# One ring of split weights for three stages, at the left end of the memory

## The chip, the cores and the metric

The kernel runs on one core of one Trainium2 chip. The metric is device time in microseconds (us) of one execution, as the median of several runs. Engines: PE (matmul), DVE (vector), ACT (scalar), POOL (GpSimd) and SP, which here only issues transfers. Each engine takes its instructions strictly in the order in which the program holds them.

## The reference, cut to what matters

One decoder layer over x of 1024 tokens by 1024 channels, all in float32:

```python
x = layer_norm(ALPHA * x + 0.5 * swiglu(x, ffn1_w_gate, ffn1_w_up, ffn1_w_down), ...)
mix = token_mixer(x, w_in, ...)          # mLSTM branch and RWKV-7 branch, merged by gates
#   inside: merged = sigmoid(gate_a) * y_a + sigmoid(gate_b) * y_b;  return merged @ w_out
x = layer_norm(ALPHA * x + mix, ln2_g, ln2_b)
x = layer_norm(ALPHA * x + 0.5 * swiglu(x, ffn2_w_gate, ffn2_w_up, ffn2_w_down), ...)
# swiglu(x, g, u, d) = (silu(x @ g) * (x @ u)) @ d, inner width 2816
```

## The kernel before

Every float32 product is made of three matmuls on numbers split into a high and a low part: a helper casts a loaded tile to its high part on ACT (L131) and subtracts that from the tile to get the low part on DVE or POOL (L135). The results go into tiles named wr. The change concerns the last three of the program's stages and the ends between them:

- D, the end of the token mixer (`mix`): each product reads split weights w or wf and is evicted by DVE (L1108, L1123), from tiles v, to DRAM (mgD).
- O, the out projection (`down_all` with w_out): three rounds over token groups (0 to 2, 3 to 5, 6 and 7), each with 8 steps. A step loads a slice of the input (hr) and two weight tiles (rw), splits them into six wr tiles, ACT for the high and DVE for the low parts, and runs 6 matmuls for each token tile in it: 18 in a step of three token tiles, 12 in the last round. At its end come the layer norms, on tiles u, and `put_sums`: PE transposes seven combinations of each finished pair of token tiles (L213), ACT and DVE split them (L216, L217) into the parts of x, the tiles xT and xq.
- the second gate stage (`gate_rest`): 22 steps f over the inner width. A step forms combinations of four weight tiles on DVE (L256, tiles tw), splits seven of them into 14 wr tiles (ACT high, POOL low), and runs seven products of 12 matmuls. The step f = 0 takes its tokens in two halves: 14 products of 12 matmuls on 256 columns. Evictions go through tiles e (DVE L277, L300, L304; ACT L288, L292, L299) to DRAM (h2, L285).
- F, the second down stage (`down_all` again): three rounds of 22 steps like those of O, then the last layer norms.

Tiles come from pools, and a pool's memory is given anew when it is closed. Left pools grow upward from low addresses, right pools downward from high ones. A tile whose memory overlaps that of older tiles waits for the last use of each of these. Which pool holds the wr ring (14 buffers of 2 KB per partition) is set by `net.wp`. Before the change there were three rings on the right: one inside O's pool, from 133.4 to 161.4 KB; one in the pool W2 of the gate stage, from 133.9 to 161.9 KB, below the e ring at 161.9 to 189.9 KB; one inside F's pool, from 137.4 to 165.4 KB. So the first ring lay partly over D's tiles v (127.9 to 139.9 KB), the second over the first and half a kilobyte of O's tile lng, the third over the second and two tiles e. In O and F `down_all` first draws one wr tile that nothing uses (`if self.wp is self.sp`).

The order of instructions on each engine, SP's transfers included, is made at build time by a scheduler that estimates when each instruction could start; so a wait for memory that the scheduler foresees also moves instructions. That the three cuts of the weights w, wf lie at 83.8 to 119.8 KB matters for the change.

Of the kernel before, what the change touches and what calls it, by code (L numbers as in the profile page):

```python
# [1134 lines left out]
def build(tc, ins, out):  # L1135
    with ExitStack() as ctx:
        net = Net(ctx, tc, ins, out)
        nc = tc.nc
        net.consts()
        x1D, x2D = (net.dp.tile([T, D], F32, tag=n, name=n) for n in ("x1D", "x2D"))  # L1140
        net.yrD, net.mbD, net.mgD = net.dram("yrD", 1024), net.dram("mbD", 1024), net.dram("mgD", 1024)
        row = lambda tt: slice(tt * P, (tt + 1) * P)

        x1T, gbb = [], []

        def hook1():
            gbb.extend((net.bcast_row(ins["ln1_g"], "lng"), net.bcast_row(ins["ln1_b"], "lnb")))
            net.consts2()

        def fin1(tt, y):  # L1150
            if tt % 4 == 0:
                x1T.append(net.new_xT())
            net.layer_norm(tt, y, *gbb, lambda t: done1(t, y))

        def done1(tt, y):
            nc.sync.dma_start(x1D[row(tt), :], y[tt])
            net.to_T(y[tt], tt, x1T)


        ctx.enter_context(net.pool("pad", "right")).tile([P, 8], F32, tag="pad", bufs=1, name="pad")  # L1160
        x, h1, h2 = ins["x"][0], net.dram("h1", DFF), net.dram("h2", DFF)
        gx, gw, xs = ExitStack(), ExitStack(), ExitStack()
        with net.rings("R1"):
            with net.pool("W1") as net.wp, net.pool("X1") as xp, net.pool("E1", "right") as net.ep:
                d = net.big(xp)
                s4 = d[:, 0:4], d[:, 4:8]
                (a22, s1), (s3, a12), (s2, a11) = (net.halves([net.big(xp) for _ in range(2)]) for _ in range(3))
                ahead = net.gate_first("ffn1", x, [a11, a12, s2, s3, s1, a22, s4], h1)
            gx.enter_context(net.shared("gx", ("xT",)))
            gw.enter_context(net.shared("gw", [t for t in net.GLOBAL if t != "xT"]))  # L1170
            with net.phase("A", UB=6, side="right"):
                net.wp = net.sp
                net.down_all(ins["ffn1_w_down"][0], NF, x, h1, fin1, hook1, ahead)

        middle(net, ins, x1T, x1D)
        gw.close()

        gb2, gb3 = [], []
        c2 = slice(0, 512), slice(512, 1024)

        def rows(v):
            return net.bcast_row(ins[v + "_g"], "lng"), net.bcast_row(ins[v + "_b"], "lnb")

        def fin2(tt, y):
            net.layer_norm(tt, y, *gb2, lambda t: done2(t, y))

        def done2(tt, y):
            nc.sync.dma_start(x2D[row(tt), :], y[tt])
            if tt % 2:
                net.put_sums(cmb, tt // 2, *([t[:, c] for c in c2] for t in y[tt - 1:tt + 1]), net.ring("tw"), "ad")  # L1190

        with net.rings("R2"):
            xp = xs.enter_context(net.pool("X2"))
            (a11, a12), (s2, s3) = (net.halves(net.new_xT()) for _ in range(2))
            s1, a22 = net.halves([net.big(xp) for _ in range(2)])
            d = net.big(xp)
            cmb = [a11, a12, s2, s3, s1, a22, (d[:, 0:4], d[:, 4:8])]
            with net.phase("O", UB=5, side="right"):
                net.wp = net.sp
                net.down_all(ins["w_out"][0], NK, x1D, net.mgD, fin2, lambda: gb2.extend(rows("ln2")))  # L1200
            with net.pool("E2", "right") as net.ep, net.pool("W2", "right") as net.wp:
                ahead = net.gate_rest("ffn2", cmb, h2, 0)
            xs.close()
            with net.phase("F", UB=6, side="right"):
                gb3.extend(rows("ln3"))
                net.wp = net.sp
                net.down_all(ins["ffn2_w_down"][0], NF, x2D, h2,
                             lambda tt, y: net.layer_norm(tt, y, *gb3, lambda t: nc.sync.dma_start(out[0, row(t), :], y[t])),
                             None, ahead)
        gx.close()  # L1210
# [93 lines left out]
```

## Time and profile before

| what | us |
|---|---|
| median of 3 runs | 3240.15 |
| lowest and highest run | 3233.46, 3247.55 |
| the profiled execution, its time | 3242.34 |
| its span, first to last instruction | 3240.3 |
| end of D to the second step of O | 2396.3 to 2405.0 |
| end of O to the second step of the gate stage | 2501.1 to 2561.7 |
| end of the gate stage to the second step of F | 2971.6 to 2987.1 |

Times of rows are us from the start of the span. A row of the timeline gives start, length, engine, line, operation, tiles written and read, and a count; in brackets the idle time before it and who ended it. Rows of matmuls overlap a little, so the pace is read from start to start. PEclk in a row of a stretch is the granted clock of PE as a share of full speed.

### The profile page before, as it was taken

What the parts mean: (1) busy time and instruction counts of PE and PEld (TensorE: products, weight loads), DVE (VectorE), ACT (ScalarE), POOL (GpSimd) and SP (SyncE); (2) the same over time, 40 slices, a digit from 0 to 9 for tenths busy, and PEclk for the clock granted to TensorE, in tenths of its full rate; (3) what the DMA queues carried; (4) which work ended last, traced back from release to release, by engine and by line L of the source; (5) the groups of instructions that cost most, each with busy time, mean ns of one, the idle gap of its engine ahead of it and who ended that gap; (6) DMA issues with size and microseconds to landing.
All of it is one profiled execution on the core that took longest, in us unless ns stands there. A gap on an engine that the chain in (4) does not pass through costs nothing. (4 is left out here: it accounts for less than half of the span.)

```text
span 3240.3 us, 45588 instructions
## 1 busy us (share of the span) xinstructions
PE 3077.5 (95%) x15888; PEld 2496.7 (77%) x15888; DVE 1908.0 (59%) x4812; ACT 1097.3 (34%) x1836; POOL 757.8 (23%) x819
## 2 busy tenths in 40 slices
PE   7999999999999999999999999999998799999997
PEld 6888878877777777787877777777776688887886
DVE  7444435583557676757667766476549544443557
ACT  4333324453213131313222222376334333332444
POOL 4444420022222222222222122200000444442000
PEclk9999999999989999999999999999999899999999
DMA  4332336662222222222232333474675232223665
GB/s 132 93 85 78 86 115 217 190 209 72 64 56 67 74 78 67 76 66 68 60 75 70 75 87 82 144 230 152 191 264 183 80 86 78 78 82 110 203 205 184
DMA packets 497389, 373.81 MB, mean 115 GB/s; under 512 B 110941, under 2 KB 415751, under 8 KB 497159
## 3 DMA queue, kind: packets, MB, share of 16 engines
q1 hardware_dynamic: 488135, 357.26, 37.2%
q0 software_dynamic: 4608, 8.39, 1.0%
q10 hardware_dynamic: 4416, 5.24, 0.5%
q8 instruction: 125, 2.05, 0.3%
q14 instruction: 105, 0.86, 0.1%
HBM read 287.43 MB, written 83.36 MB: 114 GB/s over the span
## 5 line engine op out<-in xcount | busy, mean ns | idle before, releaser
L151 PE MATMUL psg<-xT,wf 128*128 128x512 f32 x2352 | 640.6, 409 | 1.6 <-DVE h L1108 0.9
L151 PEld LDWEIGHTS psg<-xT,wf 128*128 128x128 f32 x2352 | 429.0, 191 | 78.2 <-ACT wf L131 1.3
L131 ACT CAST wr<-rw 128x512 fp32r<-128x512 f32 x444 | 273.2, 621 | 490.5 <-PE psc L151 276.7
L135 DVE TENSOR_TENSOR wr<-rw,wr 128x512 fp32r<-128x512 f32 x312 | 215.5, 697 | 197.2 <-ACT wr L131 186.5
L151 PE MATMUL psa<-xT,w 128*128 128x512 f32 x1200 | 318.5, 408 | 7.5 <-DVE pj L480 4.6
L135 POOL TENSOR_TENSOR wr<-tw,wr 128x512 fp32r<-128x512 f32 x176 | 229.9, 1308 | 248.9 <-ACT wr L131 234.9
L135 POOL TENSOR_TENSOR wr<-rw,wr 128x512 fp32r<-128x512 f32 x132 | 173.4, 1314 | 481.9 <-ACT wr L131 481.7
L151 PE MATMUL psg<-wr,wr 128*128 128x512 f32 x936 | 253.4, 398 | 23.5 <-DVE wr L135 13.3
L151 PEld LDWEIGHTS psa<-xT,w 128*128 128x128 f32 x1200 | 223.7, 193 | 59.5 <-DVE pj L480 9.3
L277 DVE TENSOR_TENSOR e<-psb,e 128x512 f32<-128x512 f32 (+1 forms) x138 | 92.1, 667 | 288.2 <-PE psb L151 288.2
L151 PE MATMUL psb<-xq,wr 128*128 128x512 f32 (+1 forms) x1104 | 257.7, 382 | 4.1 <-DVE e L277 1.7
L151 PE MATMUL psc<-xq,wr 128*128 128x512 f32 (+1 forms) x1104 | 258.7, 383 | 1.6 <-DVE e L277 1.5
L151 PE MATMUL psb<-wr,wr 128*128 128x512 f32 x936 | 250.5, 395 | 0.0
L151 PEld LDWEIGHTS psb<-xq,wr 128*128 128x128 f32 x1104 | 202.1, 189 | 45.3 <-issue 2.1
L151 PEld LDWEIGHTS psc<-xq,wr 128*128 128x128 f32 x1104 | 201.8, 188 | 44.1 <-DVE e L277 1.7
L151 PEld LDWEIGHTS psg<-wr,wr 128*128 128x128 f32 x936 | 175.8, 190 | 69.0 <-DVE wr L135 20.7
L131 ACT CAST wr<-tw 128x512 fp32r<-128x512 f32 x176 | 109.0, 621 | 307.0 <-PE psb L151 219.6
L151 PEld LDWEIGHTS psb<-wr,wr 128*128 128x128 f32 x936 | 178.1, 191 | 37.3
L135 POOL TENSOR_TENSOR w<-raw,w 128x512 fp32r<-128x512 f32 (+1 forms) x51 | 65.5, 1297 | 491.5 <-ACT w L131 429.9
L135 POOL TENSOR_TENSOR wf<-rawf,wf 128x512 fp32r<-128x512 f32 x98 | 130.0, 1342 | 169.6 <-ACT wf L131 154.0
L151 PE MATMUL psc<-wr,wr 128*128 128x512 f32 x624 | 160.1, 391 | 0.0
L758 POOL TENSOR_SCALAR S<-S,PC 128x128 f32<-128x128 f32 x120 | 80.2, 668 | 294.4 <-DVE S L760 180.5
(345 smaller groups left out, 5109.8 us busy)
## 6 DMA issues: line engine op xcount, KB each, us to landing
rw<-in_ffn_w_down_dram SPq DMA_DIRECT2D x264, 256.0 KB
rawf<-in_w_in_dram SPq DMA_DIRECT2D x98, 256.0 KB
rw<-in_ffn_w_gate_dram SPq DMA_DIRECT2D x88, 256.0 KB
rw<-in_ffn_w_up_dram SPq DMA_DIRECT2D x88, 256.0 KB
h<-e SPq DMA_DIRECT2D x80, 256.0 KB
hr<-h SPq DMA_DIRECT2D x88, 192.0 KB
raw<-in_w_in_dram SPq DMA_DIRECT2D x50, 256.0 KB
rw<-in_w_out_dram SPq DMA_DIRECT2D x48, 256.0 KB
```

The lines of the kernel that those rows point to most:

```text
L131: nc.scalar.copy(hi, src)
L135: eng.tensor_tensor(lo, src, hi.bitcast(F32), op=ALU.subtract)
L151: self.nc.tensor.matmul(out, a[u], b[v], start=first and i == 0, stop=last and i == 2, skip_group_check=more)
L277: add = lambda o, a, b: nc.vector.tensor_tensor(o, a[:, cs], b, op=ALU.add)
L758: nc.gpsimd.tensor_scalar(S1, S, pcn, None, op0=ALU.mult)
```

## The change

One wr ring, in a pool W2 opened on the left before the parts of x, serves O, the gate stage and F. It lies from 83.8 to 111.8 KB, over D's split weights w, their raw tiles, and wf; the tiles xq follow above it, from 111.8 KB. The e ring keeps its place, 161.9 to 189.9 KB. The unused tile is no longer drawn in O and F. The first stages of the program keep their addresses and their order.

```diff
-        with net.rings("R2"):
+        with net.rings("R2"), net.pool("W2") as net.wp:
             xp = xs.enter_context(net.pool("X2"))
...
             with net.phase("O", UB=5, side="right"):
-                net.wp = net.sp
                 net.down_all(ins["w_out"][0], NK, x1D, net.mgD, fin2, lambda: gb2.extend(rows("ln2")))
-            with net.pool("E2", "right") as net.ep, net.pool("W2", "right") as net.wp:
+            with net.pool("E2", "right") as net.ep:
                 ahead = net.gate_rest("ffn2", cmb, h2, 0)
             xs.close()
             with net.phase("F", UB=6, side="right"):
                 gb3.extend(rows("ln3"))
-                net.wp = net.sp
                 net.down_all(ins["ffn2_w_down"][0], NF, x2D, h2,
```

The change also moves instructions at three places. The numbers of all tiles shift by one or two.

From D to O, DVE before (v_21631 is D's last evicted tile, hr and rw the input and the weights of O's first step):

```order
L1108 TENSOR_TENSOR v_21631<-psg_21606,v_21631 128x512
L1123 TENSOR_TENSOR v_21631<-v_21631,v_21635 128x512
L135 TENSOR_TENSOR wr_21671<-hr_21664,wr_21670 128x384
L135 TENSOR_TENSOR wr_21675<-rw_21665,wr_21674 128x512
L135 TENSOR_TENSOR wr_21679<-rw_21666,wr_21678 128x512
```

and after:

```order
L1108 TENSOR_TENSOR v_21631<-psg_21606,v_21631 128x512
L135 TENSOR_TENSOR wr_21673<-hr_21666,wr_21672 128x384
L1123 TENSOR_TENSOR v_21631<-v_21631,v_21635 128x512
L135 TENSOR_TENSOR wr_21677<-rw_21667,wr_21676 128x512
L135 TENSOR_TENSOR wr_21681<-rw_21668,wr_21680 128x512
```

The first low part is made before the last eviction. By its address wr_21672 lies over a w that is long read, while wr_21673 and wr_21676 lie over wf_21564, which D's last matmul reads.

PE at the same place, before (first the last matmul of D):

```order
L151 MATMUL psg_21606<-xT_21187,wf_21564 128x512
L151 MATMUL psg_21658<-wr_21674,wr_21670 128x512
L151 MATMUL psg_21658<-wr_21675,wr_21670 128x512
L151 MATMUL psg_21658<-wr_21674,wr_21671 128x512
L151 MATMUL psg_21659<-wr_21678,wr_21670 128x512
```

and after:

```order
L151 MATMUL psg_21606<-xT_21187,wf_21564 128x512
L151 MATMUL psg_21660<-wr_21676,wr_21672 128x512
L151 MATMUL psb_21662<-wr_21676,wr_21672 128x512
L151 MATMUL psc_21664<-wr_21676,wr_21672 128x512
L151 MATMUL psg_21661<-wr_21680,wr_21672 128x512
L151 MATMUL psg_21660<-wr_21677,wr_21672 128x512
```

Four matmuls of two high parts each now stand before the first that reads a low part (wr_21677).

On SP, at this place, the loads of O's layer-norm rows and of its five tiles u (seven transfers of 512 KB) move ahead of the last two stores of mgD and of the loads for O's step 4.

From O to the gate stage, ACT before (psa to psd hold transposes of the last pair of token tiles; wr_22901 is the gate stage's first high part):

```order
L216 CAST xT_21647<-psd_22838 128x4x128
L216 CAST xT_21649<-psd_22853 128x4x128
L216 CAST xT_21649<-psa_22846 128x4x128
L216 CAST xq_21651<-psd_22868 128x4x128
L216 CAST xq_21651<-psa_22861 128x4x128
L216 CAST xq_21653<-psa_22875 128x4x128
L131 CAST wr_22901<-rw_22889 128x512
L131 CAST wr_22907<-tw_22898 128x512
L131 CAST wr_22911<-rw_22893 128x512
```

and after, where wr_22900, the first of these casts, stands still earlier, right behind the last split of O:

```order
L216 CAST xT_21650<-psd_22840 128x4x128
L131 CAST wr_22906<-tw_22897 128x512
L131 CAST wr_22910<-rw_22892 128x512
L131 CAST wr_22915<-tw_22898 128x512
L216 CAST xT_21652<-psd_22855 128x4x128
L131 CAST wr_22919<-tw_22896 128x512
L131 CAST wr_22924<-tw_22899 128x512
L216 CAST xT_21652<-psa_22848 128x4x128
L131 CAST wr_22928<-rw_22894 128x512
L216 CAST xq_21654<-psd_22870 128x4x128
L131 CAST wr_23156<-rw_23144 128x512
L216 CAST xq_21654<-psa_22863 128x4x128
```

The casts of the first weights are threaded between those of x, and POOL's low parts follow them. On PE, 12 gate matmuls now stand right behind O's last matmul, before the 14 groups of four transposes; 15 stand before the fifth last of these groups, 34 between it and the last, and 8 right behind the last. That makes 69 of the 168 matmuls of f = 0; before, all 168 stood behind the last group.

From the gate stage to F, ACT before (e_26201 to e_26207 are the last evictions, hr and rw of F's first steps):

```order
L288 COPY e_26201<-psg_26208 128x512
L292 ACTIVATE e_26202<-psg_26208 128x512
L299 ACTIVATE e_26206<-e_26206 128x512
L285 DMA h_78<-e_26205 512x1x128
L285 DMA h_78<-e_26207 512x1x128
L131 CAST wr_26324<-hr_26189 128x384
L131 CAST wr_26328<-rw_26190 128x512
L131 CAST wr_26332<-rw_26191 128x512
```

and after:

```order
L131 CAST wr_26321<-hr_26188 128x384
L288 COPY e_26200<-psg_26207 128x512
L131 CAST wr_26325<-rw_26189 128x512
L131 CAST wr_26329<-rw_26190 128x512
L292 ACTIVATE e_26201<-psg_26207 128x512
L131 CAST wr_26351<-hr_26194 128x384
L131 CAST wr_26355<-rw_26195 128x512
L131 CAST wr_26359<-rw_26196 128x512
L299 ACTIVATE e_26205<-e_26205 128x512
L285 DMA h_78<-e_26204 512x1x128
L131 CAST wr_26387<-hr_26381 128x384
L285 DMA h_78<-e_26206 512x1x128
```

The casts of F's steps 0 and 1 are threaded between the last evictions; DVE's low parts are threaded in the same way between L277, L300 and L304. The six buffers of step 0 are those of the last gate step's first three products, those of step 1 belong to its next three.

## Rows read from the trace of the kernel before

**Rows 1.** The page's first part: busy time, share of span, instructions.
```profile
PE 3077.5 (95%) x15888; PEld 2496.7 (77%) x15888; DVE 1908.0 (59%) x4812; ACT 1097.3 (34%) x1836; POOL 757.8 (23%) x819
```

**Rows 2.** Stretches: length, busy (count) of PE, PEld, DVE, ACT, POOL; clock, DMA share, GB/s.
```profile
2396.20:2405.00 8.80, 5.99 (x19) 4.54 (x19) 5.38 (x10) 4.04 (x8) 0.00 (x0) 0.81 0.67 224
2500.90:2534.90 34.00, 14.00 (x57) 9.71 (x56) 30.03 (x57) 10.92 (x18) 0.00 (x0) 0.56 0.21 78
2534.90:2561.70 26.80, 22.76 (x169) 22.06 (x170) 14.78 (x19) 9.81 (x18) 18.45 (x13) 0.92 0.30 87
2971.60:2987.00 15.40, 7.40 (x19) 5.52 (x19) 5.42 (x10) 4.04 (x8) 0.00 (x0) 0.67 0.70 210
2562.00:2970.00 408.00, 408.00 (x1758) 330.83 (x1757) 164.11 (x222) 121.52 (x205) 182.11 (x141) 1.00 0.28 80
```

**Rows 3.** Timeline of PE from D's last product to O's second step.
```profile
2390.68 5.60 PE L151 MATMUL psg<-xT,wf 128*128 128x512 f32 x24
2398.91 0.55 PE L151 MATMUL psg<-wr,wr 128*128 128x512 f32 x1 [2.63 <-ACT wr L131]
2399.64 2.50 PE L151 MATMUL psg<-wr,wr 128*128 128x512 f32 x5 [0.18 <-DVE wr L135]
...
2405.01 1.52 PE L151 MATMUL psg<-wr,wr 128*128 128x512 f32 x6
```

**Rows 4.** Timeline of DVE, then of ACT, in the same stretch.
```profile
2396.38 0.69 DVE L1108 TENSOR_TENSOR v<-psg,v 128x512 f32<-128x512 f32 x1 [4.02 <-PE psg L151]
2397.10 0.69 DVE L1123 TENSOR_TENSOR v<-v,v 128x512 f32<-128x512 f32 x1
2398.37 0.56 DVE L135 TENSOR_TENSOR wr<-hr,wr 128x384 fp32r<-128x384 f32 x1 [0.58 <-ACT wr L131]
...
2397.83 0.51 ACT L131 CAST wr<-hr 128x384 fp32r<-128x384 f32 x1 [8.47 <-DVE v L1123]
```

**Rows 5.** Timeline of PE from O's end to the gate stage's second step.
```profile
2500.02 1.08 PE L151 MATMUL psb<-wr,wr 128*128 128x512 f32 x4
2502.91 0.63 PE L213 MATMUL psa<-ident,u 128*128 128x128 f32 x4 [1.81 <-DVE u L413]
...
2532.62 1.09 PE L213 MATMUL psa<-ident,u 128*128 128x128 f32 x4 [1.84 <-DVE xq L217]
2534.91 3.86 PE L151 MATMUL psg<-xT,wr 128*128 128x256 f32 x14 [1.19 <-ACT wr L131]
...
2561.69 2.95 PE L151 MATMUL psg<-xT,wr 128*128 128x512 f32 x12
```

**Rows 6.** Timelines of ACT, DVE and POOL in that stretch.
```profile
2533.75 0.58 ACT L216 CAST xq<-psa 128x512 fp32r<-128x512 f32 x1 [2.34 <-PE psa L213]
2534.23 0.62 ACT L131 CAST wr<-rw 128x512 fp32r<-128x512 f32 x1
...
2523.87 0.68 DVE L256 TENSOR_TENSOR tw<-rw,tw 128x512 f32<-128x512 f32 x1
2537.47 1.75 DVE L256 TENSOR_TENSOR tw<-rw,rw 128x512 f32<-128x512 f32 x1 [2.42 <-POOL wr L135]
...
2534.93 1.28 POOL L135 TENSOR_TENSOR wr<-rw,wr 128x512 fp32r<-128x512 f32 x1 [278.61 <-ACT wr L131]
```

**Rows 7.** Timelines of PE, ACT and DVE from the gate stage to F.
```profile
2968.83 2.94 PE L151 MATMUL psc<-xq,wr 128*128 128x512 f32 x12
2974.95 0.50 PE L151 MATMUL psg<-wr,wr 128*128 128x512 f32 x1 [3.19 <-ACT wr L131]
2980.26 2.50 PE L151 MATMUL psg<-wr,wr 128*128 128x512 f32 x5 [4.81 <-DVE wr L135]
...
2987.07 1.55 PE L151 MATMUL psg<-wr,wr 128*128 128x512 f32 x6
...
2973.87 0.51 ACT L131 CAST wr<-hr 128x384 fp32r<-128x384 f32 x1 [3.48 <-DVE e L304]
...
2979.05 0.56 DVE L135 TENSOR_TENSOR wr<-hr,wr 128x384 fp32r<-128x384 f32 x1 [5.83 <-DMA h<-e]
```

## The prediction

> **What bounds the kernel now.** The page's first part comes first: PE is busy for 95% of the span, DVE for 59% [rows 1]. So an idle engine elsewhere is worth nothing; time can be won only where PE itself waits or runs at its lower clock. In its long stretches PE is full: the gate stage shows 408.0 us busy of 408.0 at a clock of 1.00 [rows 2]. These stretches also give the prices at full clock: 1758 matmuls of 512 columns in 408.0 us are 0.232 us each, a half-width one 0.116 us, a step of 18 matmuls 4.2 us, and the 168 half-width ones of the gate's step 0 take 19.5 us.
>
> Next come the stretches that contain the three ends which the change touches. There the granted clock is 0.81, 0.56, 0.92 and 0.67 of full speed, and PE is busy for 5.99 of 8.80, 14.00 of 34.00, 22.76 of 26.80 and 7.40 of 15.40 us [rows 2]. Then the timelines say which wait ends last at each.
>
> D to O: PE ends D at 2390.68 + 5.60 = 2396.3 and begins O's step 1 at 2405.0: 8.7 us for a step worth 4.2 [rows 3]. PE waits 2.63 us for ACT's first casts; ACT itself had waited 8.47 us for DVE's L1123, D's last eviction, though ring and v hold nothing in common but an address [rows 3, 4].
>
> O to the gate stage: from O's end at 2501.1 to the gate's step 1 at 2561.7 are 60.6 us, of which 19.5 are gate matmuls [rows 5]. No gate matmul runs before 2534.91; the first cast of its weights on ACT stands behind the last cast of x and starts at 2534.23, and POOL had been idle for 278.61 us [rows 5, 6].
>
> Gate stage to F: PE ends at 2971.8 and begins F's step 1 at 2987.1: 15.3 us for 4.2 us of work. It waits 3.19 us for ACT and 4.81 us for DVE. ACT's cast had waited for the eviction L304, DVE's first low part 5.83 us for the store of an e tile to land, because the old ring lay over e [rows 7]. After each pause PE runs slowly: five matmuls take 2.50 us, 0.50 each, against 0.232 [rows 3, 7].
>
> **The change, end by end.** Nothing is computed less. Instruction counts stay, and nothing before 2370 moves. Only waits and order change.
>
> D to O. The first high part can be cast early. The second, and the first low part, still wait for D's last matmul at 2396.3, since they lie over wf. ACT then needs one cast, 0.62 us (the size of the cast in rows 6), so the first matmul stands at about 2397.0 instead of 2398.91. The four matmuls of high parts take 0.9 us and cover DVE, which runs L1108, the first low part, L1123 and the second low part: 2396.38 + 0.69 + 0.47 + 0.65 + 0.65 gives 2398.8 [rows 4] (0.47 is the spacing behind a split of 0.56 us, 0.65 about that behind one of 0.69). The other 14 matmuls end at 2398.8 + 14 x 0.232 = 2402.0, 3.0 us earlier. That is the upper end. If the clock still falls as in [rows 3], the five slow matmuls cost 5 x 0.27 = 1.4 us, and 1.5 is left. I take 2.2, the middle. D's last eviction is delayed by 0.47 us; only its store to mgD waits for it, which O reads in its second round. On SP seven transfers of 512 KB move ahead of the loads of O's step 4: 3.7 MB at the 224 GB/s of [rows 2] are 16 us. Begun at about 2385 (DMA stands at 0.67 in this stretch), they are through by about 2402, while step 4 starts at 2402 + 3 x 4.2 = 2415. They cost nothing; without that cover they would cost a few us.
>
> O to the gate stage. Product 0's first weights are split inside O's tail, so its 12 matmuls (1.4 us) run in the gap before the first transposes, 2501.1 to 2502.91, and delay nothing [rows 5]. The chain of layer norms up to the ninth group of transposes stays. From there on the order lets 57 more matmuls run before or right behind the last group. Upper end: the last group still ends at 2532.62 + 1.09 = 2533.7; ACT and DVE split it, 0.58 us and as much again, while 8 matmuls run; the remaining 99 take 99 x 0.116 = 11.5 us, and the gate's step 1 stands at about 2546.8 instead of 2561.7: 14.9 us won. The lower end comes from DVE. With nothing on POOL its subtraction L256 takes 0.68 us; beside a POOL split it takes 1.75 [rows 6]. The change brings eight POOL splits under the stretch in which DVE forms the last parts of x, so up to eight operations there can each lose 1.07 us, and the transposes wait for them: 14.9 - 8.6 = 6.3 us. I take half of the eight, since POOL's splits are themselves spread out by ACT's order: 14.9 - 4.3 = 10.6.
>
> The Trainium skill speaks here against the change: its page GPSIMD Engine Reference, section Key points, says that GpSimd shares its SBUF interfaces with VectorE and contends with VectorE instructions that have two SBUF inputs. The trace agrees in kind, as the 1.75 against 0.68 us shows; by the rule taken strictly, with every such operation hit, this end gives 6.3 and not 10.6 us.
>
> Gate stage to F. The new ring has no e under it. Buffers of F's steps 0 and 1 come free one product after the other during the last gate step, so all of both steps but the last pair is split before PE ends at 2971.8. The first matmul can follow at once, and step 1 start at 2971.8 + 4.2 = 2976.0 instead of 2987.07: 11.1 us, with the slow clock gone as well, because the pause is. The hiding work is the last gate step, 7 products of 2.8 us each. What is queued behind a new wait: ACT's casts wait for PE to release buffers, and the last evictions L288, L292, L299 stand behind them, as L277 stands behind DVE's splits. Each such pair of splits costs the eviction at most 0.62 + 0.65 us, and PE needs the eviction only one product later. If the last two of them reach PE, 2.5 us are lost: the lower end is 8.6. I take 11, because the releases lie a full product apart.
>
> **The sum.** 2.2 + 10.6 + 11 = 23.8 us; lower ends 1.5 + 6.3 + 8.6 = 16.4, upper ends 3.0 + 14.9 + 11.1 = 29.0. The profiled execution took 3242.3, so its like would take 3218.5; it lies 2.2 us above the median of 3240.15, so the median comes to about 3216.
>
> **Rivals.**
>
> A. The lock between DVE and POOL, and PE's low clock in a thinly filled gap, eat most of the second end. For it: DVE is busy for 30.03 of 34.00 us there, and the clock is 0.56 [rows 2]. Against it: POOL's splits are only 1.28 us each and wait on ACT. Then that end gives 0 to 6 us and the total 13 to 19: about 3224.
>
> B. The change doesn't do what it says at the third end: F's first steps are held by something that the old waits hid, the loads of hr or the eviction of the last product from the accumulators. Against it: the loads of steps 0 and 1 are issued before the gate stage ends, since ACT casts them within 2 us of its release. Then about 8 of the 11 us are lost, and the time is about 3224 to 3226.
>
> C. Slower: with the pauses gone PE runs from 2397 to 3200 almost without a rest, and the chip grants it less than full clock. Price: from 2405 on some 780 us are matmul-bound, so each 0.01 of clock is 7.8 us. Below a mean clock of 0.97 there the 23.8 us are gone; at 0.95 the time is 3216 + 39 = 3255. Against it: the gate stage already runs 408 us without a pause at 1.00 [rows 2].
>
> **How the numbers follow.** The forecast, all three ends as above, has a chance of 0.62 (3211 to 3224); A 0.20, B 0.11, C 0.03, and 0.04 stay for something unseen. The runs of before lie up to 7 us from their median, so the range reaches from 3205 to 3231, which takes in A and B. A measurement of this kernel tells about 0.5%, 16.2 us, from no change: that lies at 3223.9. Nearly all of the forecast's share is faster than that, and of A and B about half: 0.78. Within 0.5%: 0.18. Slower: 0.04.
>
> **What would show it.** In the profile after, the steps 1 stand about 2.2, 13 and 24 us earlier than before. ACT no longer waits for L1123 or L304, and no DVE split for a store of e. PE shows no pause between the gate stage and F, and gate matmuls between the transposes, with POOL busy from about 2499. Wrong would be a pause of several us still standing before F, the last transposes later than 2541, or a granted clock below 1.00 in the gate stage.

## The result: 36.5 us less, 10 of them from a place without a wait

| what | before | after |
|---|---|---|
| median, us (6 runs each) | 3241.30 | 3204.76 |
| lowest and highest run | 3233.46, 3249.46 | 3203.74, 3211.45 |
| the profiled execution, its time and span | 3242.34, 3240.3 | 3204.13, 3202.1 |

The measured ratio is 0.9895, 95% interval 0.9881 to 0.9909, so 29.5 to 38.6 us were won; the two medians alone give 0.9887 and 36.5 us. The forecast was 3216 with a range from 3205 to 3231: the direction was right, the gain of 24 us too small by a third, and the median lies 0.24 us below the range.

The stretches of after that answer to [rows 2], from the same view (length, busy and count of PE, PEld, DVE, ACT, POOL; granted clock, DMA share, GB/s): D's end to O's step 1; the 34 us behind O's end; the rest up to the gate's step 1; the gate's end to F's step 1; and the gate stage:

```profile
2391.30:2397.10 5.80, 4.52 (x18) 3.41 (x19) 5.15 (x10) 3.63 (x7) 0.00 (x0) 1.00 1.03 406
2493.20:2527.20 34.00, 18.41 (x101) 14.76 (x102) 33.05 (x57) 13.02 (x22) 8.93 (x6) 0.75 0.26 91
2527.20:2544.90 17.70, 15.96 (x118) 14.45 (x118) 11.82 (x20) 6.47 (x12) 8.81 (x6) 1.00 0.34 101
2944.90:2948.80 3.90, 3.90 (x19) 3.24 (x18) 1.78 (x4) 1.13 (x2) 0.00 (x0) 1.00 0.80 236
2562.00:2930.00 368.00, 368.00 (x1625) 304.73 (x1624) 154.07 (x209) 115.55 (x194) 174.91 (x135) 1.00 0.29 84
```

The clock is 1.00 in all of them but the second, which has 0.75; [rows 2] had 0.81, 0.56, 0.92 and 0.67 in the first four. The last row holds the surprise. Before, 1758 matmuls filled 408.00 us, 0.232 each; now 1625 fill 368.00, 0.2265 each. PE is full and at the same clock in both, and the instructions are the same.

To compare all kernels below, I measured each profile in one way: **end 1** from the end of D's last matmul to O's 19th matmul (its step 1); **end 2** from O's last matmul to the gate's step 1 (the start of that step's second product, less 2.72 us for the first, since its first product is now threaded among step 0); **the gate stage**, steps 1 to 21; **end 3** from its end to F's 19th matmul. O itself (96.1 us), F behind its step 0 (239.1) and the tail (14.2) are the same in all kernels, within 0.4 us.

| kernel | D's end | end 1 | end 2 | gate stage | end 3 |
|---|---|---|---|---|---|
| before | 2396.3 | 8.7 | 60.7 | 410.0 | 15.3 |
| after | 2391.3 | 5.8 | 51.7 | 400.0 | 3.9 |
| won | | 2.9 | 8.9 | 10.0 | 11.4 |

These make 33.2 us. The other 5.0 of the 38.2 between the two spans lie ahead of D's end, in code that the change does not touch: over all profiles here D's end varies from 2382.8 to 2401.2. So parts are compared from D's end on, and medians with their intervals; the 33.2 us lie inside that of the result.

**End 1** answers to [rows 3, 4]. The timeline of after, PE first, then ACT (start, length; in brackets the idle time before and who ended it):

```profile
2385.67 5.60 PE L151 MATMUL psg<-xT,wf 128*128 128x512 f32 x24
2391.98 0.50 PE L151 MATMUL psg<-wr,wr 128*128 128x512 f32 x1 [0.71 <-ACT wr L131]
2392.32 0.40 PE L151 MATMUL psb<-wr,wr 128*128 128x512 f32 x1
...
2393.78 0.73 PE L151 MATMUL psg<-wr,wr 128*128 128x512 f32 x2 [0.60 <-DVE wr L135]
...
2397.12 1.52 PE L151 MATMUL psg<-wr,wr 128*128 128x512 f32 x6
...
2385.02 0.50 ACT L131 CAST wr<-hr 128x384 fp32r<-128x384 f32 x1
2391.31 1.14 ACT L131 CAST wr<-rw 128x512 fp32r<-128x512 f32 x2 [5.79 <-PE psg L151]
```

The first cast stands 6 us ahead of D's end, the second waits for D's last matmul, PE waits 0.71 and 0.60 us instead of 2.63 and 0.18, and it starts its second matmul 0.34 us behind the first: the slow matmuls of [rows 3], 0.50 each, are gone.

**End 2** answers to [rows 5, 6]. PE, then DVE, then POOL of after:

```profile
2492.10 1.08 PE L151 MATMUL psb<-wr,wr 128*128 128x512 f32 x4
...
2519.92 0.39 PE L151 MATMUL psb<-xT,wr 128*128 128x256 f32 x1 [1.17 <-POOL wr L135]
...
2524.98 0.39 PE L151 MATMUL psc<-xq,wr 128*128 128x256 f32 x1 [1.56 <-POOL wr L135]
...
2529.54 0.66 PE L213 MATMUL psa<-ident,u 128*128 128x128 f32 x4 [0.68 <-DVE xq L217]
...
2491.37 1.25 DVE L163 TENSOR_TENSOR rst<-lnr 128x2 f32<-128x2 f32 x1
...
2518.06 0.68 DVE L225 TENSOR_TENSOR u<-u,u 128x512 f32<-128x512 f32 x1
2518.66 1.75 DVE L256 TENSOR_TENSOR tw<-rw,tw 128x512 f32<-128x512 f32 x1
2520.34 1.77 DVE L227 TENSOR_TENSOR u<-tw,u 128x512 f32<-128x512 f32 x1
2522.04 1.76 DVE L256 TENSOR_TENSOR tw<-rw,rw 128x512 f32<-128x512 f32 x1
2523.72 0.68 DVE L217 TENSOR_TENSOR xT<-psd,xT 128x512 fp32r<-128x512 f32 x1
...
2518.27 1.59 POOL L135 TENSOR_TENSOR wr<-tw,wr 128x512 fp32r<-128x512 f32 x1 [25.67 <-ACT wr L131]
```

From 2518.27, when POOL's splits begin, DVE's operations whose two inputs both lie in SBUF, the memory of the tiles spoken of so far, take up to 1.77 us instead of 0.68, while L217, which reads one input from PSUM, the memory of PE's results (psa to psg), keeps 0.68. The last transposes stand 36.4 us behind O's end (2493.18), against 31.5 before.

**End 3** answers to [rows 7]: PE, then ACT.

```profile
2942.04 2.88 PE L151 MATMUL psc<-xq,wr 128*128 128x512 f32 x12
2944.76 1.52 PE L151 MATMUL psg<-wr,wr 128*128 128x512 f32 x6
...
2948.84 1.52 PE L151 MATMUL psg<-wr,wr 128*128 128x512 f32 x6
...
2939.33 0.62 ACT L131 CAST wr<-rw 128x512 fp32r<-128x512 f32 x1 [2.20 <-PE psc L151]
```

F's first matmul follows the gate's last without a pause; a cast of F's weights waits for one product to release its buffer, no longer for L304 or for a store of e.

### The profile page after: what moved, and what is told of

Its sections match the earlier page's. It is cut to its first block, busy times and chain, and to the rows that moved or that the text cites. A ratio compares the mean times of both kernels' runs of the same rounds, so it can differ in the third digit from the quotient of the medians.

```text
span 3202.1 us, 45591 instructions
## 1 busy us (share of the span) xinstructions
PE 3056.9 (95%) x15888; PEld 2486.7 (78%) x15888; DVE 1909.5 (60%) x4812; ACT 1098.2 (34%) x1836; POOL 761.8 (24%) x819
## 5 line engine op out<-in xcount | busy, mean ns | idle before, releaser
L277 DVE TENSOR_TENSOR e<-psb,e 128x512 f32<-128x512 f32 (+1 forms) x138 | 92.1, 668 | 270.5 <-PE psb L151 270.5
```

What stands on the lines that cost most here:

```text
L277: add = lambda o, a, b: nc.vector.tensor_tensor(o, a[:, cs], b, op=ALU.add)
```

## The experiments

### Why do the gate's matmuls run faster?

Three theories. *Place*: it matters whether the ring lies above or below the parts of x. *Offset*: it matters where the weights begin against the tile that streams past them, within some small unit of bytes. In the kernel before, all parts of x begin 1856 bytes past a multiple of 2 KB and the gate's ring 1984, so the ring was 128 bytes off; in the kernel after both begin at 1856. *Execution*: the pace changes from run to run. Four kernels separate them.

**p1**, the kernel before with the gate's ring 128 bytes lower:

```diff
-            with net.pool("E2", "right") as net.ep, net.pool("W2", "right") as net.wp:
+            with net.pool("E2", "right") as net.ep, net.pool("P2", "right") as p2, net.pool("W2", "right") as net.wp:
+                p2.tile([P, 32], F32, tag="pad2", bufs=1, name="pad2")
```

> The kernel before, with one edit: an unused tile of 128 bytes is drawn ahead of the gate stage's ring, so that this ring begins at 133.81 and not 133.94 KB; it stays on the right, above all parts of x, and the three rings stay apart. In the kernel before the parts of x lie 1856 bytes past a multiple of 2 KB and the gate's ring 1984, in the kernel after both 1856. In the profile of before a matmul of the second gate stage takes 0.2325 us from start to start, in the one after 0.2267, over 21 steps some 10 us that the prediction did not have. Theory 'offset' (the pace hangs on where in 2 KB the weights lie against x): 0.2267, the gate stage's 21 steps take 400 us instead of 410, the time falls by about 10 us to 3231 (ratio 0.997). Theory 'place' (the pace hangs on the ring being above or below the parts of x): 0.2325, the time stays (1.000). Theory 'execution' (the pace changes from one execution to the next): either, with no relation to the edit.

Measured: median 3227.0, ratio to before 0.995 (0.9933 to 0.9968). The same stretch of the gate stage by the view of stretches, before and then p1:

```profile
2600.00:2900.00 300.00, 300.00 (x1292) 243.26 (x1291) 125.10 (x170) 91.86 (x154) 138.36 (x108) 1.00 0.29 84
```

```profile
2600.00:2900.00 300.00, 300.00 (x1325) 248.41 (x1324) 126.66 (x174) 94.16 (x158) 143.37 (x111) 1.00 0.29 85
```

In 300 us PE does 1325 matmuls instead of 1292. The gate stage takes 400.0 us, the three ends stay at 8.6, 60.7 and 15.1. An unused tile of 128 bytes wins the 10 us; *place* is out for this pair, since the ring stays above x.

**p2**, the kernel after with the ring 128 bytes higher, so that xT (below it) is off and xq (above it, moved along) is not:

```diff
-        with net.rings("R2"), net.pool("W2") as net.wp:
+        with net.rings("R2"), net.pool("P2") as p2, net.pool("W2") as net.wp:
+            p2.tile([P, 32], F32, tag="pad2", bufs=1, name="pad2")
```

> The kernel after, with one edit: an unused tile of 128 bytes lies ahead of the shared ring, so that the ring and the tiles xq above it begin 1984 bytes past a multiple of 2 KB, while the tiles xT stay at 1856. The ring stays between xT and xq on the left. Theory 'offset': the four products of a gate step that read xT slow down to 0.2325 us for a matmul, the three that read xq keep 0.2267; over the stage 10 x 4/7 = 5.8 us are lost, time about 3210.5 (1.002 of after, 0.991 of before). Theory 'place': all seven products keep 0.2267 and the time stays at about 3205 (0.989). Theory 'execution': either pace, but for all seven products alike. The three ends as in the kernel after in any case.

Measured: median 3212.81, ratio to before 0.9911 (0.989 to 0.9932). The timeline of PE, five products of 12 matmuls; the pace is read from start to start:

```profile
2712.45 2.96 PE L151 MATMUL psb<-xT,wr 128*128 128x512 f32 x12
2715.24 2.90 PE L151 MATMUL psc<-xq,wr 128*128 128x512 f32 x12
2717.98 2.88 PE L151 MATMUL psb<-xq,wr 128*128 128x512 f32 x12
2720.70 2.88 PE L151 MATMUL psc<-xq,wr 128*128 128x512 f32 x12
2723.42 2.96 PE L151 MATMUL psg<-xT,wr 128*128 128x512 f32 x12
```

Within one gate step the products on xT take 2.79 to 2.80 us and the last two on xq 2.72 (the first of them 2.74). That rules out *execution*, and the clock with it: the pace changes every few us with the tile that is read. The stage takes 406.8 us, 6.8 more than after. The 5.8 expected went by a slow pace of 0.2325 us a matmul; here it is up to 0.2333 (2.80 for a product of 12).

**r1 and r2**, the shared ring on the right (161.9 to 189.9 KB, with e below it), in r2 with 128 unused bytes ahead:

```diff
-        with net.rings("R2"), net.pool("W2") as net.wp:
+        with net.rings("R2"), net.pool("W2", "right") as net.wp:
```

```diff
-        with net.rings("R2"), net.pool("W2") as net.wp:
+        with net.rings("R2"), net.pool("P2", "right") as p2, net.pool("W2", "right") as net.wp:
+            p2.tile([P, 32], F32, tag="pad2", bufs=1, name="pad2")
```

> The kernel after, with the one shared ring opened on the right instead of on the left: it lies from 161.9 to 189.9 KB, e below it from 133.9 to 161.9 KB, and all parts of x adjoin from 19.8 to 131.8 KB as in the kernel before. Nothing of D's split weights lies under the ring, so O's first splits no longer wait for D's last matmul. The ends O to gate and gate to F should stay as in the kernel after (52 and 4 us), D to O be no longer than its 5.85 us, down to 4.2. Theory 'offset' and theory 'place' both: the gate stage's matmuls take 0.2325 us, 10 us are given back, time about 3213 to 3215 (0.992 of before). If the pace came from sharing one ring, or from the pauses being gone, it stays at 0.2267 and the time is 3203 to 3205 (0.989). Against the prediction's sum, which had no such term, 3241 - 24 = 3217.

> The shared ring on the right as in r1, with 128 unused bytes ahead of it, so that it lies 1856 bytes past a multiple of 2 KB like all parts of x. Theory 'offset': the gate stage's matmuls run at 0.2267 as in the kernel after, D to O stays at r1's 4.2 us (after: 5.85), the other two ends at 52 and 4: 1.7 us less than after, about 3203 (0.9995 of after, 0.988 of before), and some 11 us less than r1. Theory 'place' (a ring above all of x is slow): 0.2333 and 3214 to 3216 as r1.

Measured: r1 3216.3, ratio to before 0.9931 (0.991 to 0.9952); r2 3207.57, 0.9896 (0.9879 to 0.9913). The stretch of r1, then of r2:

```profile
2600.00:2900.00 300.00, 300.00 (x1287) 241.36 (x1286) 125.14 (x171) 91.77 (x154) 138.66 (x107) 1.00 0.28 80
```

```profile
2600.00:2900.00 300.00, 300.00 (x1325) 248.43 (x1324) 127.23 (x174) 94.05 (x158) 143.39 (x111) 1.00 0.29 84
```

Same place, both above all of x: slow when 128 bytes off, full when not. (In r2 the e ring moves by 128 bytes too; in p1 the wr ring alone does.) The gate stage takes 411.7 and 400.0 us. So r1, which has all that the change was meant to bring, falls 11.7 us behind in the gate stage by its offset. Ends 2 and 3 are those of after in r1 (51.7, 3.9), and nearly so in r2 (52.1, 3.9). End 1 is 4.2 in both: nothing of D's split weights lies under this ring, so all of O's first splits are ready when D ends.

**a0**, the kernel after once more, beside r2:

> The kernel after, unchanged, on the same chip as r2, for the comparison of the two, and for its pace in a second execution: by theory 'offset' 0.2267 again, 3204 to 3206; by theory 'execution' it may be 0.2325.

Measured: 3207.01, ratio 0.9892 (0.9874 to 0.991), gate stage 400.0, ends 5.8, 51.8 and 3.9. The pace is the same in a second execution. r2 wins 1.7 us at end 1, loses 0.4 at end 2, and its median can't be told from that of a0: no complete version here beats the kernel after.

**s1 and s2**, the kernel after with three unused tiles, which put three different offsets into one profile. The sizes in bytes are 64, 128, 128 in s1 and 32, 512, 512 in s2:

```diff
+        with net.rings("R2"), net.pool("P2") as p2, net.pool("W2") as net.wp:
+            p2.tile([P, 16], F32, tag="pad2", bufs=1, name="pad2")
...
+            xp.tile([P, 32], F32, tag="pad3", bufs=1, name="pad3")
             s1, a22 = net.halves([net.big(xp) for _ in range(2)])
+            xp.tile([P, 32], F32, tag="pad4", bufs=1, name="pad4")
             d = net.big(xp)
```

> The kernel after with three small unused tiles: 64 bytes ahead of the ring, 128 between the ring and the first two tiles xq, 128 ahead of the third. Against the ring, xT then lies 64 bytes lower, the first two xq 128 bytes higher and the third 256 higher (all modulo 2 KB). In a gate step four products read xT (into psg, psb, psg, psb), two the first two xq (psc, psb) and one the third (psc), so one profile gives the pace at three offsets. Known so far: 0.2267 us a matmul at offset 0, 0.2324 to 0.2333 at 128 bytes with the ring higher. If any offset costs, all seven products take over 0.231; if the sign of the offset counted, the two at +128 would run at 0.2267; if only a whole number of some larger unit is free, the one at 256 runs at 0.2267 and xT at 64 is slow.

> As the last one, with unused tiles of 32, 512 and 512 bytes: against the ring, xT lies 32 bytes lower, the first two xq 512 bytes higher, the third 1024 higher. Which of these offsets runs at 0.2267 and which at 0.231 or above tells the unit: if any offset within 2 KB costs, all are slow; if the unit is 512, only xT is slow; if a step of 32 is too small to matter, xT runs at 0.2267.

One execution each (3217.49 and 3202.44 us; the two times are no comparison, since D ends 11.8 us apart in them). The timeline of PE in s1:

```profile
2712.87 2.96 PE L151 MATMUL psb<-xT,wr 128*128 128x512 f32 x12
2715.67 2.95 PE L151 MATMUL psc<-xq,wr 128*128 128x512 f32 x12
2718.46 2.94 PE L151 MATMUL psb<-xq,wr 128*128 128x512 f32 x12
2721.24 2.93 PE L151 MATMUL psc<-xq,wr 128*128 128x512 f32 x12
2724.01 2.96 PE L151 MATMUL psg<-xT,wr 128*128 128x512 f32 x12
```

and in s2:

```profile
2705.34 2.88 PE L151 MATMUL psb<-xq,wr 128*128 128x512 f32 x12
2708.06 2.88 PE L151 MATMUL psc<-xq,wr 128*128 128x512 f32 x12
2710.78 2.96 PE L151 MATMUL psg<-xT,wr 128*128 128x512 f32 x12
2713.59 2.96 PE L151 MATMUL psb<-xT,wr 128*128 128x512 f32 x12
```

| offset of x against the ring, bytes | a product of 12, us | from |
|---|---|---|
| 0 | 2.72 | after, p1, r2 |
| -32 | 2.80 | s2, xT |
| -64 | 2.80 | s1, xT |
| -128 | 2.78 to 2.80 | before, r1, p2 |
| +128 | 2.78 to 2.79 | s1, first two xq |
| +256 | 2.77 | s1, third xq |
| +512 | 2.72 (2.74 behind a product on xT, as in p2) | s2, first two xq |
| +1024 | 2.72 | s2, third xq |

So every offset tried that is no multiple of 512 bytes costs 2 to 3%, 32 bytes lower as much as 128 lower, 128 or 256 bytes higher a little less; 512 and 1024 cost nothing. The offset does not set the slow pace alone: before and r1 both have -128, and their gate stages take 410.0 and 411.7 us; what makes these 1.7 us no run shows. 512 bytes is what one partition of a 128-column weight tile holds in float32. That this is the reason, and what PE waits for, no run shows.

The Trainium skill, page SBUF — State Buffer, section "SBUF: two separate sides", says that on the engines' side only the port pair of DVE and GpSimd contends and that PE never waits on anyone. The rows of p2 neither bear this out nor speak against it: they show products slowed from 2.72 to 2.80 us by where a tile lies, with no wait on another engine, and not whether any other engine holds PE up.

### What limits end 2?

Theory: the lock, as the prediction calls it (DVE's operations last longer beside POOL's), the lower end of its second term. Rival: PE's low clock and DVE's own work. **n1** leaves out POOL's low parts of the gate's step 0, **n2** (`f < 2`) those of steps 0 and 1; PE, ACT and DVE keep their work.

```diff
         hl = self.ring("wr"), self.ring("wr")
-        self.split(t, *hl)
+        if getattr(self, "nolow", False):
+            self.nc.scalar.copy(hl[0], t)
+            hl = hl[0], hl[0]
+        else:
+            self.split(t, *hl)
...
+            self.nolow = f0 == 0 and f == 0
             ws = self.weights(*(self.raws(pre, f, 0) + self.raws(pre, f, 1)))
+            self.nolow = False
```

> The kernel after, but in step 0 of the second gate stage POOL forms no low parts: the matmuls that would read them read the high parts again, so PE, ACT and DVE keep their work and POOL has none until step 1; the output lacks the products with those low parts. It tells what the lock between POOL and DVE takes of the end O to gate, forecast at 4.3 us of at most 14.9, of which about 8.9 were won. Theory (the lock is the term that was mis-sized): with POOL idle, DVE's L256, L227 and L230 in this end fall back from 1.2 to 1.8 us to 0.5 to 0.8, and the gate's step 1 starts 4 to 6 us earlier, time about 3200 (0.9975 of after). Rival (DVE's own work and PE's low clock fill the end): under 1.5 us earlier, time 3203.5 to 3205.

> As n1, but POOL forms no low parts in the steps 0 and 1 of the second gate stage; in n1 POOL's splits of step 1 still fell on DVE's last four L256 (0.97 to 1.78 us), and PE still waited 2.00 us for an eviction on DVE behind them. From O's end to the start of the gate's step 1 (counted as the start of its second product less one product) after takes 51.7 us and n1 48.9; before took 60.6, and the upper end of the prediction (no lock, no slow clock) was 45.7. If the lock is all that was missing, 45.7 to 46.7; if PE's low clock and DVE's own work take the rest, 48 to 49.

Measured: end 2 is 48.9 us in n1 and 46.2 in n2, against 51.7 in after; medians 3202.64 (0.9887 of before, 0.9867 to 0.9906) and 3202.68 (0.9886, 0.986 to 0.9911). The medians can't tell the two apart; the traces can, since end 2 repeats to 0.1 us in after, a0, p2, r1, s1, s2 and f1. In n2, DVE (L260 is L256 of the other kernels), then PE:

```profile
2520.52 0.69 DVE L260 TENSOR_TENSOR tw<-rw,tw 128x512 f32<-128x512 f32 x1
2521.12 0.68 DVE L227 TENSOR_TENSOR u<-tw,u 128x512 f32<-128x512 f32 x1
...
2527.02 0.65 PE L213 MATMUL psa<-ident,u 128*128 128x128 f32 x4
```

Operations that took 1.75 and 1.77 us are back at 0.69 and 0.68, and the last transposes stand 31.1 us behind O's end (2495.93), against 36.4 in after and 31.5 before the change. n1 met neither theory (2.9 us, between its 4 to 6 and 1.5): its last transposes are back at 31.4 us, but POOL's splits of step 1 then fell on DVE's combinations around and behind them, which took up to 1.78 us, and PE waited 2.00 us for an eviction behind these. n2 takes those splits away too. Without POOL's work the end is 51.7 - 46.2 = 5.5 us shorter, and wins 60.7 - 46.2 = 14.5.

n2 also takes away PE's own waits for POOL's low parts, 1.17 and 1.56 us in after, which is a rival for the 5.5. The trace of after speaks for the lock: the last transposes wait for DVE's L217, DVE has no idle time in the 15 us before them, and its operations lose 4.7 us there and 1.1 in L163, enough for the 5.3 us by which the transposes move.

**v2 and v3** try to win some of that: the combinations of weights L256 of step 0 (v2), or of steps 0 and 1 (v3), go from DVE to POOL.

```diff
-        sub = lambda o, a, b: self.nc.vector.tensor_tensor(o, a, b, op=ALU.subtract)
+        eng = self.nc.gpsimd if getattr(self, "subpool", False) else self.nc.vector
+        sub = lambda o, a, b: eng.tensor_tensor(o, a, b, op=ALU.subtract)
...
+            self.subpool = f0 == 0 and f == 0
             ws = self.weights(*(self.raws(pre, f, 0) + self.raws(pre, f, 1)))
+            self.subpool = False
```

> The kernel after, with the five combinations of weights of step 0 of the second gate stage formed by POOL instead of DVE (five of the L256 in the end O to gate, 0.68 to 1.77 us each beside POOL's splits); nothing is left out. If DVE, slowed by the lock, sets the last transposes (36.7 us after O's end; 31.5 without POOL's work), taking five operations of 0.7 to 1.8 us off it brings them forward by up to 5 us and step 1 by 1 to 3 us, time about 3202 to 3204. Rival: POOL, with five more operations of 1.3 to 1.7 us on it and each locking DVE's remaining ones, becomes the late one: the products' low parts come later and the end is 52 us or longer, time 3205 to 3209.

> As v2, with the combinations of step 1 on POOL too: all L256 of the end are off DVE, ten more operations are on POOL. By the theory, up to 2 us more than v2; by the rival, POOL is some 14 us busier in a stretch of 40 us and step 1 waits for its low parts: 53 to 58 us from O's end, time 3206 to 3211.

Measured: 3207.69, 0.9905 of before (0.9882 to 0.9929), and 3210.97, 0.992 (0.9897 to 0.9943). End 2 grows to 57.3 and 57.0 us, and the last transposes stand 41.9 and 41.6 us behind O's end. The rival was right. In v3 (whose L257 is L256 of the others), PE, then DVE, then POOL:

```profile
2527.91 2.29 PE L151 MATMUL psc<-xq,wr 128*128 128x256 f32 x9 [4.63 <-POOL wr L135]
...
2520.82 1.67 DVE L227 TENSOR_TENSOR u<-tw,u 128x512 f32<-128x512 f32 x1
...
2520.24 1.70 POOL L257 TENSOR_TENSOR tw<-rw,tw 128x512 f32<-128x512 f32 x1
```

POOL needs 1.3 to 1.7 us, once 2.25, for what DVE does in 0.68, and is late itself now; the transposes stand in PE's queue behind the matmuls that wait 4.63 us for it.

### Is end 3 a matter of the memory under F's ring?

**f1**, the kernel after with a ring of F's own, over xq and two tiles e:

```diff
                 gb3.extend(rows("ln3"))
+                net.wp = net.sp
```

> The kernel after, but F gets a ring of its own again, inside its pool from 137.4 to 165.4 KB; O and the gate stage keep the shared ring on the left. F's ring now lies over xq (111.8 to 159.8 KB), which the gate stage's matmuls read to the end, and over two tiles e. Theory (the third end comes from the memory under F's ring): the pause between the gate stage and F returns, and since nearly all of the ring waits for the last products, it is at least the 15.3 us of before (from the gate's end to F's step 1; after: 3.9), up to 19; the first two ends and the pace of 0.2267 stay; time 3216 to 3221 (1.0035 to 1.005 of after, 0.993 of before). Rival (the pause had gone because of the shared order or the missing unused tile, not the memory): 3.9 us and 3205.

Measured: 3214.09, 0.9917 of before (0.9893 to 0.9941); ends 5.8, 51.7 and 11.0, gate stage 400.0. The pause is back, but at 7.1 of the 11.4 us. My "at least 15.3" was wrong. PE, ACT and DVE:

```profile
2944.61 2.88 PE L151 MATMUL psc<-xq,wr 128*128 128x512 f32 x12
2950.63 0.80 PE L151 MATMUL psg<-wr,wr 128*128 128x512 f32 x1 [3.13 <-ACT wr L131]
2952.87 2.50 PE L151 MATMUL psg<-wr,wr 128*128 128x512 f32 x5 [1.44 <-DVE wr L135]
...
2949.54 0.51 ACT L131 CAST wr<-hr 128x384 fp32r<-128x384 f32 x1 [3.37 <-DVE e L304]
...
2951.65 0.56 DVE L135 TENSOR_TENSOR wr<-hr,wr 128x384 fp32r<-128x384 f32 x1 [2.70 <-DMA h<-e]
```

The chain is that of [rows 7], ACT behind L304 and DVE behind a store of e; only the store's landing ends 2.70 us of waiting and not 5.83. Why it lands earlier no run tries; in before, two loads of layer-norm rows (L191) go out at 2971.80 and 2972.17, just ahead of the last store at 2973.25, and in f1 at 2944.58 and 2944.96, 4 us ahead of it at 2948.98. f1 draws the unused tile again too; that memory makes this end is seen from whom the first splits wait for, an eviction and a store of e, with which they share nothing else. How much it costs differs: 11.4 us in before, 7.1 in f1.

## Why the prediction was right, and where it was short

- **The three ends.** 2.9, 8.9 and 11.4 us against 2.2, 10.6 and 11 make 23.2 against 23.8: the sum of the terms was right within 0.6 us. That it is so close is partly luck, since the second term was 1.7 too large and the other two 0.7 and 0.4 too small.
- **End 1.** The upper end (3.0) came true. The middle was taken for fear that five matmuls stay slow; the clock is 1.00 there and none is.
- **End 2.** The upper end, 14.9, is 14.5 by n2. (As the terms are written, 2533.7 + 2 x 0.58 + 11.5 is 2546.3 and not 2546.8, so 15.3 and not 14.9; and in end 1, 3.0 - 1.4 leaves 1.6 and not 1.5.) The lock was forecast at half of eight operations, 4.3 us, and costs 5.5. In after, six operations of DVE ahead of the last transposes lose 0.47 to 1.09 us each, and L163 on two columns loses 1.10 beside the single POOL split in O's tail. The rule that the prediction took from the Trainium skill, page GPSIMD Engine Reference, section Key points, taken strictly, gave 8.6 us; the runs lie between, nearer to the half. That POOL would be busy from about 2499 on was wrong: it does one split at 2491 and then waits 25.67 us for ACT.
- **End 3.** The mechanism is as forecast, and 11.4 us lie a little above the upper end of 11.1; the evictions behind the casts cost PE nothing.
- **The step that failed** is the sentence on prices: "1758 matmuls of 512 columns in 408.0 us are 0.232 us each" was taken as what a matmul costs at full clock. It was the pace of one placement. O's steps and F's in the same trace run at 0.2267, and so do the products of 12 in the first gate stage; I did not lay one against the other; "Nothing is computed less" then left no place for a gain inside the stage. The missing term is 21 steps x 84 matmuls x 0.0057 us = 10 us, which p1, p2, r1 and r2 show to be the offset. With it the sum is 33.8, and 3242.3 less that 3208.5. In the trace of before, two products of 12 of the first gate stage, 2.72 us apart, and a group of 6 of O's step 1, 1.36 us behind the one at 2405.01 in [rows 3]:

```profile
204.71 2.88 PE L151 MATMUL psb<-xq,wr 128*128 128x512 f32 x12
207.43 2.88 PE L151 MATMUL psc<-xq,wr 128*128 128x512 f32 x12
...
2406.37 1.52 PE L151 MATMUL psb<-wr,wr 128*128 128x512 f32 x6
```

- **Rivals.** A: the lock is there, but takes 5.5 of the 14.5, not most. B: none of it. C: the clock is 1.00 from O's step 1 on but for end 2. None foresaw that the ring's place decides the pace. r1, which has the three ends without it, is 24 us faster than before by the medians, the size of the forecast; by its trace it wins 24.8 us at the ends, 4.5 of them at end 1, and loses 1.7 in the gate stage.

## What to carry to other kernels

When two stages run the same instruction at the same granted clock, compare its pace from start to start between them: a difference of 2% that no wait explains is a place to win, here 10 us by an unused tile of 128 bytes. Where a change moves buffers, look at what lies under each new address (whose last use it will wait for) and at how weights and streamed tiles stand to each other within 512 bytes. Before work is moved under a busy stretch of DVE, price what POOL does beside it: here it took back 5.5 of 14.5 us.

## What the hardware showed that was not expected

A float32 matmul of 512 columns took 0.2267 us when its weights and its streamed tile began at the same byte within 512, and 0.231 to 0.2333 us at each of the other offsets tried, at a granted clock of 1.00 and with no wait in the trace. And a DVE operation on two columns, L163, took 1.25 us instead of 0.15 beside one POOL split.
